# One engine for the norms', the output projections' and the second MLP matrix's adds, and two latent pairs ahead of the context

## The chip, the cores and the metric

One of the eight cores of one Trainium2 chip runs the kernel. Its engines each work through a queue of their own in order: TensorE (PE; PEld is its weight load), VectorE (DVE), ScalarE (ACT), GpSimd (POOL) and SyncE (SP), which issues the DMAs. The metric is the time of one execution on the device in microseconds; less is better. The median of three runs is given, and rows come from one profiled execution.

## What is computed

Two layers of a diffusion trunk over 1024 latent tokens and 256 context tokens, width 1024, all in float32. Layer 0 mixes by multi-head latent attention, layer 1 by gated linear attention (GLA). Cut to what matters here:

```python
for i in range(2):
    h_lat, h_ctx = modulated rms_norm of x_lat, x_ctx
    y_ctx, y_lat = mixer(h_ctx, h_lat)          # ends with "@ w_o", the output projection
    x_lat = x_lat + m_lat[:, 2] * rms_norm(y_lat, norm_g[i, 1])
    h = modulate(rms_norm(x_lat, norm_g[i, 2]), m_lat[:, 3], m_lat[:, 4])
    x_lat = x_lat + m_lat[:, 5] * rms_norm(sqrelu_mlp(h, w1[i], w2[i]), norm_g[i, 3])
    # in layer 0 the same two lines for x_ctx
def sqrelu_mlp(h, w1, w2):
    return jnp.square(jax.nn.relu(h @ w1)) @ w2   # hidden width 4096
```

## The kernel before

**Data and matmuls.** Activations lie transposed, a tile for each 128 of the 1024 channels: 128 partitions by 256 context tokens (block 0) or 512 latent tokens (blocks 1 and 2). Each float32 product is three matmuls (`mm3`, L234 to L236: high x high, high x low, low x high). Each operand is therefore split in two: ScalarE casts the high part (L204), and VectorE or GpSimd subtracts it for the low part (L201), by the engine that the call names; `alternate()` takes the two in turn. A tile's name tells its pool: `stg` and `s` come by DMA, `w` holds weight splits, `m` and `c` activations of 512 and 256 columns, `t` short-lived ones, `ps` is PSUM.

**What sets the order.** The program is written in Python for a framework that orders the instructions of each engine when it is built, by a simulated timeline, and puts in the waits. On the chip each engine keeps to that order.

**Stages.** Attention of layer 0 runs to about 700 us. The output projection (`out_proj`, `out_items`, L796 to L815; blocks 1, 0, 2) lasts to 842. For each half of the output channels it runs over eight input tiles, splits operand and weight (L804, L805) and issues the matmuls for four PSUM tiles. Then it copies each (L812), and `sumsq` (L294 to L302) squares it on ScalarE (L301) and adds it up (L302), here on GpSimd. Each block's norm, `residual_norm_steps` (L846 to L885), runs in the background behind the next block's matmuls. It calls `rstd` (L304 to L320; L309 is the matmul with ones that sums over the partitions), multiplies eight tiles by gate and rstd (L860), adds the residual (L862), stores the stream (L866, L868), squares and sums again (L301, L302), calls `rstd` once more and modulates (`modulate`, L326 to L329, or L880 with `whole`). Which engine adds at L862 is said by a table, `PLAN['radd']`, that names the tiles that go to VectorE; the others go to GpSimd.

**The first MLP matrix.** `mlp` (L891) splits the eight tiles of the latent block 1 (L898 on), waits until the context block is ready (`ready(h[0])`), and issues eight early pairs in layer 0, eleven in layer 1, by `up_early` (L975): two Strassen products of a latent pair (`top_left`), then, in layer 0, two products on the context (`up_ctx_part`). The other products follow in `up_pair`, from about 940 in layer 0.

**The second MLP matrix.** `down` (L1057 to L1149) lasts from 1215 to about 1565 in layer 0, and from 2600 to 2860 in layer 1. It is a Strassen product in five stages of sixteen steps each. A step has four `mm3`, with weights prepared two steps ahead. The weights of the stages are combinations of four blocks of the matrix, kept in one tile for each pair of rows: `s3` and `s1` in the first two stages, `w_s1` and `w_s2` in the next two, each with one add or subtract (L889) on GpSimd and a split on VectorE. `sums`, at the end of the fourth stage, has four adds for each of four output tiles, two of them on GpSimd. `ada_halves` (L268) runs between the steps. `into_ctx` (L1233) adds context products from PSUM. After `down` come `down_tail` and the norm of the block, in layer 0 from 1565 to 1680.

**GLA.** It runs from 1680 to 2250. Its output projection (`gla_wo`) and the norms of its two blocks run from about 2240, and the early pairs of layer 1 from 2318. The last norm of all lies within 2860 to 2997.

## Time and profile before

| | before |
|---|---|
| median of 3 runs | 3007.78 us (3006.51 to 3010.25) |
| profiled execution | 2998.72 us, span 2996.9 us |
| granted clock of TensorE, mean | 0.963 |
| TensorE (PE) | 2767.2 us busy, 92% |
| VectorE (DVE) | 2293.1 us, 77% |
| ScalarE (ACT) | 1599.5 us, 53% |
| GpSimd (POOL) | 1484.2 us, 50% |
| DMA | 179 GB/s mean |

The page gives busy time of each engine over the whole span. A row of the timeline has the start in us after the span's start, the time to the end of the last of its instructions, engine, line, operation, output and inputs, the shape, the count, and in brackets the idle time of the engine ahead of it and what ended that. In the tables by stage a row has the window and its length, then busy us and, in brackets, instructions of PE, PEld, DVE, ACT and POOL, then the granted clock, the DMA engines' busy share and GB/s. The two windows of the section below are the loops of the second MLP matrix in layer 0 and in layer 1. The granted clock is 1.00 for 2.4 GHz and 0.50 for 1.2 GHz.

### The profile page before, as it was taken

What the parts mean: (1) busy time and instruction counts of PE and PEld (TensorE: products, weight loads), DVE (VectorE), ACT (ScalarE), POOL (GpSimd) and SP (SyncE); (2) the same over time, 40 slices, a digit from 0 to 9 for tenths busy, and PEclk for the clock granted to TensorE, in tenths of its full rate; (3) what the DMA queues carried; (4) which work ended last, traced back from release to release, by engine and by line L of the source; (5) the groups of instructions that cost most, each with busy time, mean ns of one, the idle gap of its engine ahead of it and who ended that gap; (6) DMA issues with size and microseconds to landing.
All of it is one profiled execution on the core that took longest, in us unless ns stands there. A gap on an engine that the chain in (4) does not pass through costs nothing. (4 is left out here: it accounts for less than half of the span.)

```text
span 2996.9 us, 44715 instructions
## 1 busy us (share of the span) xinstructions
PE 2767.2 (92%) x14646; PEld 2360.5 (79%) x14646; DVE 2293.1 (77%) x3776; ACT 1599.5 (53%) x3360; POOL 1484.2 (50%) x1029
## 2 busy tenths in 40 slices
PE   6799898999889989999999999799888989999997
PEld 4678787898778778888777888688777768788877
DVE  8898999886898985576888683466898876576676
ACT  5577576665455334444435454656655644555433
POOL 5554444425634753332533252366565389664522
PEclk8999999999899999999999999899999999999999
DMA  5221334225554874487755465666576547577454
GB/s 205 69 80 58 125 109 137 90 76 175 176 172 158 262 243 144 149 286 227 237 187 173 164 204 170 213 213 226 191 261 203 197 156 238 172 270 255 146 186 144
DMA packets 319386, 535.49 MB, mean 179 GB/s; under 512 B 33073, under 2 KB 96433, under 8 KB 319153
## 3 DMA queue, kind: packets, MB, share of 16 engines
q1 hardware_dynamic: 313328, 527.39, 53.6%
q10 hardware_dynamic: 5760, 5.25, 0.5%
q8 instruction: 115, 1.88, 0.3%
q14 instruction: 119, 0.97, 0.1%
q0 software_dynamic: 64, 0.00, 0.0%
HBM read 412.18 MB, written 120.32 MB: 178 GB/s over the span
## 5 line engine op out<-in xcount | busy, mean ns | idle before, releaser
L235 PE MATMUL ps<-m,w 128*128 128x512 f32 (+1 forms) x2320 | 907.4, 392 | 25.9 <-DVE m L201 24.6
L236 PE MATMUL ps<-m,w 128*128 128x512 f32 (+1 forms) x2320 | 903.0, 392 | 29.1 <-DVE w L201 23.4
L234 PE MATMUL ps<-m,w 128*128 128x512 f32 (+1 forms) x2320 | 893.2, 394 | 28.5 <-ACT m L204 11.8
L235 PEld LDWEIGHTS ps<-m,w 128*128 128x128 f32 x2320 | 447.7, 193 | 124.7 <-DVE m L201 33.9
L236 PEld LDWEIGHTS ps<-m,w 128*128 128x128 f32 x2320 | 446.1, 193 | 124.4 <-DVE w L201 29.5
L234 PEld LDWEIGHTS ps<-m,w 128*128 128x128 f32 x2320 | 444.9, 192 | 122.9 <-ACT m L204 16.5
L204 ACT CAST w<-stg 128x512 fp32r<-128x512 f32 (+2 forms) x510 | 308.6, 613 | 273.1 <-PE ps L235 205.1
L201 POOL TENSOR_TENSOR w<-stg,w 128x512 fp32r<-128x512 f32 (+2 forms) x173 | 241.7, 1399 | 382.2 <-ACT w L204 315.6
L201 DVE TENSOR_TENSOR w<-stg,w 128x512 fp32r<-128x512 f32 x337 | 308.8, 923 | 155.9 <-ACT w L204 142.0
L204 ACT CAST m<-stg 128x512 fp32r<-128x512 f32 x296 | 177.7, 623 | 180.7 <-DMA stg<-hid 162.6
L201 DVE TENSOR_TENSOR m<-stg,m 128x512 fp32r<-128x512 f32 x220 | 199.5, 928 | 60.3 <-ACT m L204 60.0
L234 PE MATMUL ps<-m,m 128*128 128x256 f32 (+1 forms) x632 | 187.9, 317 | 28.1 <-ACT m L204 17.8
L235 PE MATMUL ps<-m,m 128*128 128x256 f32 (+1 forms) x632 | 196.1, 312 | 11.5 <-POOL m L201 7.2
L234 PE MATMUL ps<-c,w 128*128 128x256 f32 (+1 forms) x664 | 185.6, 286 | 15.6 <-ACT c L436 7.0
L236 PE MATMUL ps<-m,m 128*128 128x256 f32 (+1 forms) x632 | 192.5, 306 | 1.8 <-DVE m L427 1.8
L235 PE MATMUL ps<-c,w 128*128 128x256 f32 (+1 forms) x664 | 186.0, 284 | 6.1 <-DVE c L437 3.5
L236 PE MATMUL ps<-c,w 128*128 128x256 f32 (+1 forms) x664 | 185.7, 284 | 0.1
L965 ACT ACTIVATE t<-t 128x512 f32<-128x512 f32 x109 | 68.8, 631 | 204.8 <-DVE t L889 194.9
L889 DVE TENSOR_TENSOR t<-ps,t 128x512 f32<-128x512 f32 x164 | 111.1, 684 | 79.9 <-PE ps L236 54.6
L889 POOL TENSOR_TENSOR m<-stg,stg 128x512 f32<-128x512 f32 x64 | 95.3, 1495 | 131.2 <-DVE w L201 64.4
L234 PEld LDWEIGHTS ps<-m,m 128*128 128x128 f32 x632 | 124.2, 197 | 38.9 <-ACT m L204 19.3
L889 POOL TENSOR_TENSOR t<-t,t 128x512 f32<-128x512 f32 x82 | 123.4, 1513 | 39.8 <-issue 19.2
(312 smaller groups left out, 6490.1 us busy)
## 6 DMA issues: line engine op xcount, KB each, us to landing
stg<-in_mlp_w SPq DMA_DIRECT2D x256, 256.0 KB, 3.9
stg<-hid SPq DMA_DIRECT2D x227, 256.0 KB, 3.7
hid<-t SPq DMA_DIRECT2D x205, 256.0 KB, 3.3
stg<-in_w SPq DMA_DIRECT2D x182, 256.0 KB, 3.0
ada<-in_adaT SPq DMA_DIRECT2D x88, 512.0 KB, 3.6
stg<-in_adaT SPq DMA_DIRECT2D x112, 256.0 KB, 3.6
stg<-in_gla_wv SPq DMA_DIRECT2D x64, 256.0 KB, 3.7
stg<-in_mla_wo SPq DMA_DIRECT2D x48, 256.0 KB, 4.1
```

What stands on the lines that cost most here:

```text
L201: eng.tensor_tensor(out=out, in0=a, in1=bits(hi), op=ALU.subtract)
L204: self.nc.scalar.copy(hi, src)
L234: mm(ps, lhs[0], rhs[0], start=first, stop=False, skip_group_check=shared)
L235: mm(ps, lhs[0], rhs[1], start=False, stop=False, skip_group_check=shared)
L236: mm(ps, lhs[1], rhs[0], start=False, stop=last, skip_group_check=shared)
L889: eng.tensor_tensor(out=out, in0=a, in1=b, op=op)
L965: self.nc.scalar.activation(c, c, AF.Relu)
```

## The change

Four edits. (1) In `out_items` both splits' subtracts and the square-sums go to VectorE, in place of taking turns and of GpSimd (4 calls: 48 subtracts, 28 square-sums; `out_half_items`, the other form of gla_wo, stays). (2) All residual adds of `residual_norm_steps` are VectorE's; the table is gone (52 move). (3) In `down` the adds of `s3`, `s1`, `w_s1` and `w_s2` are VectorE's (64 in each layer), and `sums` leaves only its first add in place. The three others go into a list, and each of the following steps issues one, on VectorE (16 in both layers move engine). (4) `up_early` is cut in two. The latent part, `up_first`, is called for two pairs ahead of the wait for the context block, and their context parts, `up_first_ctx`, come after it, in the loop as before. VectorE has 3995 instructions of its program's queue after, 3724 before; GpSimd 762 and 1034.

```diff
- 'radd': [[6, 7], [6], [6, 7, 1, 2], [6, 7, 5]],
+ 'ahead': 2,
...
@@ out_items
-                    o.append(self.msplit(self.load(src[k, :, t0 - off:t0 - off + w]), w, self.alternate()))
-                ww = self.weight(self.I[wname][k * P:(k + 1) * P, half * 512:half * 512 + 512], self.alternate())
+                    o.append(self.msplit(self.load(src[k, :, t0 - off:t0 - off + w]), w, self.nc.vector))
+                ww = self.weight(self.I[wname][k * P:(k + 1) * P, half * 512:half * 512 + 512], self.nc.vector)
...
-                self.sumsq(acc, pss[n], half == 0 and n == 0, w, self.nc.gpsimd)
+                self.sumsq(acc, pss[n], half == 0 and n == 0, w)
@@ residual_norm_steps
-            (nc.vector if k in PLAN['radd'][l * 2 + (gate == 5)] else nc.gpsimd).tensor_tensor(out=ys[k], in0=ys[k], in1=xs[k], op=ALU.add)
+            nc.vector.tensor_tensor(out=ys[k], in0=ys[k], in1=xs[k], op=ALU.add)
@@ mlp
+        hc = h[0] if ctx else None
...
+        ahead = PLAN["ahead"] if ctx else 0
+        held = [self.up_first(l, p, ops) for p in range(ahead)]
         if ctx:
             self.ready(h[0])
...
         for p in range(early):
-            self.up_early(l, p, ops, hc)
+            w = held.pop(0) if held else self.up_first(l, p, ops)
+            self.up_first_ctx(l, p, w, hc)
@@ up_early, now up_first and up_first_ctx
+        return w
+
+    def up_first_ctx(self, l, p, w, hc):
         if hc:
+            V = self.nc.vector
             self.up_ctx_part(2 * p, (w["11"], w["12"]), hc)
             self.up_ctx_part(2 * p + 1, [self.weight(self.I["w1"][l, 2 * p + 1, i], V) for i in range(2)], hc)
@@ down
-            self.tt(Pl, keep[p], a11, part(p, 0, 1), ALU.subtract)
+            self.tt(V, keep[p], a11, part(p, 0, 1), ALU.subtract)
...
-            self.tt(Pl, keep[p], keep[p], part(p, 0, 0), ALU.subtract)
+            self.tt(V, keep[p], keep[p], part(p, 0, 0), ALU.subtract)
...
-            self.tt(Pl, C["u3", n], C["u3", n], u, ALU.add)
-            self.tt(Pl, u, u, C["22", n], ALU.add)
-            self.tt(V, C["22", n], C["22", n], C["u3", n], ALU.add)
+            later.extend(((C["u3", n], C["u3", n], u), (u, u, C["22", n]), (C["22", n], C["22", n], C["u3", n])))
...
             if p % 3 == 0:
                 self.ada_halves(1)
+            if later:
+                self.tt(V, *later.pop(0), ALU.add)
```

Three places in the order of the instructions; a name is a pool's letter with two running numbers.

TensorE at the end of the output projection of layer 0, before (ps2355 is its last tile, m2384 the sum of squares of the context block, m2410 and m2411 the first latent operand of the MLP):

```order
L234 MATMUL ps2355_9632<-m2339_9586,w2398_9833 128x512
L235 MATMUL ps2355_9632<-m2340_9587,w2398_9833 128x512
L236 MATMUL ps2355_9632<-m2339_9586,w2399_9834 128x512
L309 MATMUL ps2426_9914<-m2384_9770,ones_70 128x256
L234 MATMUL ps2460_9985<-m2410_9882,w2453_9973 128x512
L235 MATMUL ps2460_9985<-m2411_9883,w2453_9973 128x512
L236 MATMUL ps2460_9985<-m2410_9882,w2454_9974 128x512
```

and after, from the same tile on:

```order
L234 MATMUL ps2355_9632<-m2339_9586,w2398_9833 128x512
L235 MATMUL ps2355_9632<-m2340_9587,w2398_9833 128x512
L236 MATMUL ps2355_9632<-m2339_9586,w2399_9834 128x512
L234 MATMUL ps2434_9928<-m2410_9882,w2427_9916 128x512
L234 MATMUL ps2435_9942<-m2418_9898,w2430_9922 128x512
L234 MATMUL ps2444_9974<-m2410_9882,w2437_9962 128x512
L234 MATMUL ps2445_9988<-m2418_9898,w2440_9968 128x512
L235 MATMUL ps2434_9928<-m2411_9883,w2427_9916 128x512
```

and 44 rows later:

```order
L234 MATMUL ps2445_9988<-m2424_9910,w2440_9968 128x512
L235 MATMUL ps2445_9988<-m2425_9911,w2440_9968 128x512
L236 MATMUL ps2445_9988<-m2424_9910,w2441_9969 128x512
L309 MATMUL ps2446_10006<-m2384_9770,ones_70 128x256
L234 MATMUL ps2472_10063<-c2449_10017,w2427_9916 128x256
L234 MATMUL ps2480_10104<-c2449_10017,w2475_10094 128x256
```

48 matmuls of the two latent pairs stand between the projection and L309 now, and the first matmul on a context operand (c2449) comes right behind L309.

VectorE at the norm of latent block 2 behind the second MLP of layer 0, before, from the seventh of the eight L860 on (m3325 is a context product that `into_ctx` adds to, w4163 a weight split of `down_tail`):

```order
L860 SCALAR_TENSOR_TENSOR m3881_16384<-m3881_16384,m005_80,m4133_17357 128x512
L860 SCALAR_TENSOR_TENSOR m3882_16389<-m3882_16389,m005_80,m4133_17357 128x512
L889 TENSOR_TENSOR m3325_14241<-m3325_14241,ps4151_17461 128x256
L201 TENSOR_TENSOR w4163_17496<-stg4155_17481,w4162_17495 128x512
L201 TENSOR_TENSOR w4209_17712<-stg4203_17701,w4208_17711 128x512
```

and after:

```order
L860 SCALAR_TENSOR_TENSOR m3881_16384<-m3881_16384,m005_80,m4133_17357 128x512
L860 SCALAR_TENSOR_TENSOR m3882_16389<-m3882_16389,m005_80,m4133_17357 128x512
L889 TENSOR_TENSOR m3325_14241<-m3325_14241,ps4151_17461 128x256
L201 TENSOR_TENSOR w4163_17496<-stg4155_17481,w4162_17495 128x512
L862 TENSOR_TENSOR m3999_16834<-m3999_16834,s4128_17335 128x512
L862 TENSOR_TENSOR m4000_16839<-m4000_16839,s4129_17337 128x512
L201 TENSOR_TENSOR w4209_17712<-stg4203_17701,w4208_17711 128x512
L862 TENSOR_TENSOR m4001_16844<-m4001_16844,s4130_17339 128x512
L862 TENSOR_TENSOR m4002_16849<-m4002_16849,s4131_17341 128x512
```

The eight L860 keep their place, and four residual adds (L862) now come in VectorE's queue, behind the context's L889 and the split w4163.

VectorE at the norm behind gla_wo, before, from the seventh of its eight L860 on (w6143 is a weight split of gla_wo):

```order
L860 SCALAR_TENSOR_TENSOR m5973_24727<-m5973_24727,m102_88,m6078_25170 128x512
L860 SCALAR_TENSOR_TENSOR m5975_24732<-m5975_24732,m102_88,m6078_25170 128x512
L862 TENSOR_TENSOR m5888_24375<-m5888_24375,s6068_25138 128x512
L862 TENSOR_TENSOR m5890_24380<-m5890_24380,s6069_25140 128x512
L201 TENSOR_TENSOR w6143_25419<-stg6141_25416,w6142_25418 128x512
L302 TENSOR_TENSOR m6091_25225<-m6091_25225,t6094_25237 128x512
L302 TENSOR_TENSOR m6091_25225<-m6091_25225,t6102_25269 128x512
```

and after:

```order
L860 SCALAR_TENSOR_TENSOR m5973_24727<-m5973_24727,m102_88,m6078_25170 128x512
L860 SCALAR_TENSOR_TENSOR m5975_24732<-m5975_24732,m102_88,m6078_25170 128x512
L862 TENSOR_TENSOR m5887_24372<-m5887_24372,s6067_25136 128x512
L862 TENSOR_TENSOR m5888_24375<-m5888_24375,s6068_25138 128x512
L201 TENSOR_TENSOR w6143_25419<-stg6141_25416,w6142_25418 128x512
L862 TENSOR_TENSOR m5890_24380<-m5890_24380,s6069_25140 128x512
L862 TENSOR_TENSOR m5892_24385<-m5892_24385,s6070_25142 128x512
L201 TENSOR_TENSOR w6148_25446<-stg6146_25443,w6147_25445 128x512
```

Two residual adds stand ahead of w6143 both times: before those of the second and third tile (m5888, m5890), now those of the first and second. The next two stand behind it now; the one of the fourth tile (m5892) was GpSimd's.

## Rows read from the trace of the kernel before

**Rows 1.** The page: busy us of an engine, share of the span, instructions.

```profile
PE 2767.2 (92%) x14646; PEld 2360.5 (79%) x14646; DVE 2293.1 (77%) x3776; ACT 1599.5 (53%) x3360; POOL 1484.2 (50%) x1029
```

**Rows 2.** Table by stage: window, busy us of PE, PEld, DVE, ACT, POOL, clock, DMA.

```profile
1215.00:1565.00 350.00, 338.32 (x1712) 287.54 (x1711) 257.82 (x444) 151.98 (x289) 137.79 (x92) 0.98 0.69 225
...
2600.00:2860.00 260.00, 260.00 (x1149) 215.29 (x1148) 177.19 (x205) 127.01 (x220) 140.96 (x95) 1.00 0.65 218
```

**Rows 3.** Timelines of DVE and POOL where the other is idle: start, us, instruction.

```profile
794.63 1.07 DVE L812 COPY m<-ps 128x256 f32<-128x256 f32 x3
795.63 0.68 DVE L862 TENSOR_TENSOR m<-m,s 128x512 f32<-128x512 f32 x1
796.23 0.68 DVE L201 TENSOR_TENSOR w<-stg,w 128x512 fp32r<-128x512 f32 x1
...
2337.61 5.38 DVE L860 SCALAR_TENSOR_TENSOR m<-m,m,m 128x512 f32<-128x512 f32 x8
...
2343.07 1.29 POOL L862 TENSOR_TENSOR m<-m,s 128x512 f32<-128x512 f32 x1 [16.68 <-DVE m L860]
```

**Rows 4.** Timelines of DVE and POOL at the norms and the sums, where both work.

```profile
774.93 11.52 DVE L860 SCALAR_TENSOR_TENSOR m<-m,m,m 128x512 f32<-128x512 f32 x8
...
1531.56 6.81 DVE L201 TENSOR_TENSOR m<-stg,m 128x512 fp32r<-128x512 f32 x4
...
1590.04 12.53 DVE L860 SCALAR_TENSOR_TENSOR m<-m,m,m 128x512 f32<-128x512 f32 x8
1595.29 8.41 POOL L862 TENSOR_TENSOR m<-m,s 128x512 f32<-128x512 f32 x5
...
2274.46 10.59 DVE L860 SCALAR_TENSOR_TENSOR m<-m,m,m 128x512 f32<-128x512 f32 x8
2288.33 1.75 DVE L201 TENSOR_TENSOR w<-stg,w 128x512 fp32r<-128x512 f32 x1
...
2358.06 1.30 DVE L862 TENSOR_TENSOR m<-m,s 128x512 f32<-128x512 f32 x1 [1.82 <-DMA s<-x_scr]
...
2898.02 12.64 DVE L860 SCALAR_TENSOR_TENSOR m<-m,m,m 128x512 f32<-128x512 f32 x8
```

**Rows 5.** Timeline of PE: its idle time ahead of the row in brackets.

```profile
804.82 2.04 PE L309 MATMUL ps<-m,ones 128*128 128x512 f32 x2 [4.37 <-DVE m L302]
...
854.72 1.22 PE L309 MATMUL ps<-m,ones 128*128 128x256 f32 x2 [13.14 <-DVE m L302]
...
1602.95 0.58 PE L234 MATMUL ps<-c,w 128*128 128x256 f32 x1 [6.90 <-DVE m L889]
...
2290.14 1.22 PE L236 MATMUL ps<-m,w 128*128 128x512 f32 x2 [4.29 <-DVE w L201]
...
2323.63 0.80 PE L235 MATMUL ps<-m,w 128*128 128x512 f32 x1 [3.62 <-DVE m L201]
...
2364.57 2.08 PE L309 MATMUL ps<-m,ones 128*128 128x512 f32 x2 [4.41 <-DVE m L302]
...
2912.38 0.58 PE L235 MATMUL ps<-m,w 128*128 128x512 f32 x1 [2.88 <-DVE m L201]
```

**Rows 6.** Table by stretch, four intervals at half clock, columns as in rows 2.

```profile
803.20:810.00 6.80, 5.18 (x10) 3.48 (x11) 3.78 (x4) 2.87 (x5) 3.76 (x3) 0.50 0.72 239
...
1598.50:1608.80 10.30, 5.85 (x21) 5.35 (x22) 10.30 (x14) 3.61 (x7) 6.05 (x5) 0.50 0.66 198
2288.00:2294.80 6.80, 4.66 (x11) 3.69 (x12) 6.59 (x5) 3.39 (x6) 6.59 (x4) 0.50 0.89 286
...
2912.70:2916.10 3.40, 3.40 (x9) 2.65 (x8) 3.40 (x7) 0.92 (x2) 0.00 (x0) 0.50 0.70 202
```

**Rows 7.** Timeline of PE: first matmul on context operands of the first MLP.

```profile
862.20 0.40 PE L234 MATMUL ps<-c,w 128*128 128x256 f32 x2
```

**Rows 8.** Waits of PE from 1420 to 1620: us in total, times, longest us.

```profile
PE ps L235 <- DVE m L201: 10.5, 4, 5.3
```

**Rows 9.** Waits of POOL from 1200 to 1600, columns as in rows 8.

```profile
POOL m L889 <- DMA stg<-in_mlp_w: 50.5, 14, 13.1
```

More of the change, by code (lines that the diff above doesn't have):

```diff
@@ L897, in mlp @@
             ops["11" if k < 4 else "21"].append(self.msplit(h[1][k], 512, self.nc.vector))
+        hc = h[0] if ctx else None
+        second = self.strassen_y(ops, h[1], h[2])
+        ahead = PLAN["ahead"] if ctx else 0
+        held = [self.up_first(l, p, ops) for p in range(ahead)]
         if ctx:
             self.ready(h[0])
-        hc = h[0] if ctx else None
-        second = self.strassen_y(ops, h[1], h[2])
         for p in range(early):
-            self.up_early(l, p, ops, hc)
+            w = held.pop(0) if held else self.up_first(l, p, ops)
+            self.up_first_ctx(l, p, w, hc)
             self.tick(PLAN["etick"][l])
@@ L973, in top_left, with up_first @@
         return a, c
-    def up_early(self, l, p, B, hc):
+    def up_first(self, l, p, B):
         V = self.nc.vector
@@ L1064, in down @@
         nc = self.nc
-        Pl, V = nc.gpsimd, nc.vector
-        keep = {}
+        V = nc.vector
+        keep, later = {}, []
         def part(p, r, i):
@@ L1072, in s3 @@
             keep[p] = self.m()
-            self.tt(Pl, keep[p], a11, part(p, 0, 1), ALU.subtract)
+            self.tt(V, keep[p], a11, part(p, 0, 1), ALU.subtract)
         def s1(p, a21):
-            self.tt(Pl, keep[p], a21, part(p, 1, 1), ALU.add)
+            self.tt(V, keep[p], a21, part(p, 1, 1), ALU.add)
         def w_first(p):
@@ L1096, in w_s2 @@
             w = self.wsplit(keep[p], V)
-            self.tt(Pl, keep[p], part(p, 1, 0), keep[p], ALU.subtract)
+            self.tt(V, keep[p], part(p, 1, 0), keep[p], ALU.subtract)
             return w, None
```

## The prediction

> **What bounds the kernel now.** I read the page first. TensorE is busy 92% of the span [rows 1], so what can be won without removing matmuls is its idle time, some 230 us, and the stretches after an idle time in which its clock is at half. VectorE is busy 77%. The table by stage comes next. In the second MLP product of layer 1 TensorE is busy for all 260 us while VectorE has 177 us of work, and in that of layer 0 it is 338 of 350 with VectorE at 258 [rows 2]. So there is room on VectorE in those stages, and in layer 1 nothing can be won.
>
> Then the timelines of VectorE and GpSimd, side by side. A run of eight L860 takes 5.38 us where GpSimd is idle, 0.67 apart, and instructions with two operands of 512 columns start 0.60 apart (795.63, 796.23), copies of 256 columns 0.33 apart (three in 1.07) [rows 3]. The same eight L860 take 10.6 to 12.6 us where GpSimd adds the residuals beside them, and five such GpSimd adds take 8.41, so 1.68 each, against 1.29 for one alone [rows 4]. So the two engines hold each other up: while both work on SBUF operands, VectorE does in 1.5 us what it does in 0.6 to 0.7 alone. An add moved from GpSimd to VectorE then costs VectorE 0.60, and saves the 0.9 that its neighbours lost to it.
>
> Last the idle times of TensorE, row by row, with what ended them [rows 5]. Seven are 2.9 to 13.1 us long, all seven were ended by VectorE, and all lie in or right behind an output projection or a residual norm. Behind them the granted clock is 0.50, the lower of its two levels (1.2 GHz of 2.4): in the four intervals shown for 3.4 to 10.3 us. What that costs is half of TensorE's busy time in it: 2.6, 2.9, 2.3 and 1.7 us [rows 6].
>
> **The change part by part.** It moves 272 instructions from GpSimd to VectorE: 48 subtracts and 28 square-sums of the output projections, 52 residual adds, 144 adds of the second MLP product. It removes none, and TensorE and ScalarE keep theirs (one instruction more in TensorE's queue, at nothing).
>
> *Output projections, layer 0.* The idle time of 4.37 us at 804.82 ends with the second norm's sum [rows 5]. Its last square-sum is on VectorE behind 11.5 us of L860. In the new order 42 instructions stand from the first L860 to that sum, eight at 0.67, 26 at 0.60, eight of 256 columns at 0.33: (5.4 + 15.6 + 2.6) = 23.6 us from 774.9, so 798.5, ahead of 804.82 − 4.37 = 800.45, where TensorE ran out. Idle time and half clock go: 4.4 + 2.6 = 7.0 saved. The shorter wait at the start of that block stays, since the queue before the operand gained as many instructions as each got shorter.
>
> *Two latent pairs ahead.* The idle time of 13.14 at 854.72 is TensorE waiting with L309 for the sum over the context block, with the first MLP's matmuls queued behind [rows 5]. In the new order 48 matmuls of the two pairs stand ahead of it (48 x 0.226 = 10.9 us, by 1149 matmuls in 260 us [rows 2]). But they wait for the operand splits of the latent block, and these stand in VectorE's queue behind six instructions of 512 columns and five of 256, (6 x 0.60 + 5 x 0.33) = 5.3 us. And then the context's chain, from L309 at 854.72 to the first matmul on context operands at 862.20, 7.5 us [rows 5, 7], lies open: today 24 latent matmuls run inside it, and these have been used up. Less the first sum itself and what the chain loses to splits that stand between its steps today, 5.5 to 6.5 us of it are idle. So 5.3 ahead and some 6 behind take the place of 13.14: −2. With the wait in two pieces there may be a second half-clock stretch, so I take no clock gain here. If the operands come sooner than I count, the bound is the whole 13.1 plus 1.5 of clock.
>
> *Second MLP, layer 0.* 72 adds move to VectorE: 258 + 72 x 0.60 = 301 us of 350, before what the missing contention gives back, so it doesn't become the bound by load. Four waits for VectorE's operand splits, 10.5 us in all, the longest 5.3 [rows 8]. The 5.3 is that of the sums at the end of the product: now four L889, then splits at 1.7 each (three in 5.11) beside GpSimd's adds [rows 4]; then four plus three L889 and two splits, 9 x 0.60 = 5.4. Nothing won there. The other three, 5.2 in all, sit behind contended splits; I take 3 of it and 1.5 of clock (below the smallest interval of rows 6, as two of the three are short): −4.5.
>
> *Residual norm of the layer-0 MLP.* The largest: 6.90 idle at 1602.95, ended by L889 (into_ctx) that stands behind the eight L860 of 12.53 us [rows 4, 5]. In the new order the eight L860 stand alone, 8 x 0.67 = 5.4, to which two GpSimd splits of the tail's weights may still add 0.9 each. L889 then ends at 1590.04 + 5.4 + 1.8 + 0.4 = 1597.6, TensorE ran out at 1596.05. So 5.3 to 6.9 of idle time and the clock's 2.9 go: −8.5.
>
> *Layer 1: gla_wo and norms.* w6143, the weight split for which TensorE waits 4.29 us, runs at 2288.33, behind eight L860 of 10.59 and two adds [rows 4, 5]. After: one more split, eight at 0.67, two at 0.60 and its own 0.68 from 2274.46, so 2282.3, before TensorE runs out at 2290.14 − 4.29 = 2285.85: 4.3 + 2.3 of clock = −6.6. The wait of 3.62 at 2323.63 is for operand splits beside GpSimd square-sums, which move: −1. The one of 4.41 at 2364.57 looks alike, but the add at 2358.06 was itself waiting for the load of the residual (1.82, DMA) [rows 4], and that load comes when an earlier add frees its buffer. Earlier adds bring it forward by 2 us, not more: −2. At the last norm eight L860 take 12.64 and the operand split behind them is 2.88 late [rows 4, 5]: −2.9 − 1.7 = −4.6. The second MLP of layer 1 is full on TensorE, with 177 + 43 of 260 on VectorE afterwards [rows 2]: nothing.
>
> *What may come in its place.* An add on GpSimd that waits (for a residual or a weight by DMA) held up only GpSimd's queue. On VectorE it holds up the operand splits behind it, and TensorE after them. GpSimd's adds of the second MLP in layer 0 waited 50.5 us for weights by DMA, in 14 waits [rows 9]. The bounds are 0 (VectorE gets to them later than GpSimd did, the data is there) and 50.5. VectorE is at 301 of 350 and TensorE's work is prepared two steps ahead, so I am near the lower end: +6.
>
> Sum: −7.0 − 2 − 4.5 − 8.5 − 6.6 − 1 − 2 − 4.6 = −36.2, and +6: **−30 us**. The profiled execution took 2998.7 in its own time, and the median of three is 9 us above it; the difference is put on the median: 3007.8 − 30 = **2978**.
>
> **A rule that speaks against it.** The rows have VectorE's instructions of 0.68 us start 0.60 apart, one behind the other [rows 3]. The Trainium skill (VectorE: DVE Perf Modes, "The DRAIN you can't avoid") says that each VectorE instruction is followed by a drain of about its duration less 266 ns before the next starts, but also that one which isn't held starts earlier. By the first half an instruction would take 0.68 + 0.41 = 1.09, the 144 adds of the second MLP 157 us in place of 86, and the sum would be about −30 + 71 = +41. The trace doesn't agree with that pace, so the sum stays as it is.
>
> **The rivals.** (1) *Half of it comes.* The waits lie in VectorE's one queue, and an earlier L860 only exposes the next wait: a residual's load (as at 2358.06), a ScalarE cast, a square. For it: the wait at 2364.57 is of that kind already. Against: for the largest terms the queue is counted through, and the loads are not late there. Then −15, 2993. (2) *VectorE inherits GpSimd's waits* in the layer-0 second MLP: the adds stand in its queue ahead of the splits, and wait for weights. If most of the 50.5 us reaches TensorE, the time is 3007.8 − 30 + 50.5 = 3028; it decides once more than 36 of the 50.5 come through, from there on the kernel is slower by over 6. Against it: TensorE has two prepared steps, 5.4 us, ahead, and the 14 waits are 3.6 us on average. (3) *Nothing that can be measured*: the half above, and a few waits of rival 2 (12 us) beside it, 3005. (4) *VectorE doesn't run the moved adds at 0.60.* Other GpSimd work moves up beside them, and each holds VectorE for some 1.1 us, between the 0.60 of rows 3 and the 1.5 of rows 4: the 144 adds of the second MLP cost 72 us more, layer 1's stage included (177 + 79 of 260), and the time is 3049. The drain of the Trainium skill would give the same; the pace in rows 3 is against it.
>
> **How the numbers follow.** About 0.2% (6 us) is what a measurement of this kernel can tell from no change. Forecast, 2978: 0.60, its own range 2955 to 2989. Half, 2993: 0.22. No difference, 3005: 0.08. Slower by GpSimd's inherited waits, 3028: 0.09; by adds at 1.1 us, 0.01. The lower bound is the sum without the +6 and with the whole of the 13.1 and its clock: −36.2 − 12.6 = −49, and 5 for splits that run free in stretches I didn't count: 2953. The upper end takes in the half gain with some loss, up to 3002; what lies above is 0.15, below 0.05. Faster 0.82, same 0.08, slower 0.10.
>
> **What would show it.** Runs of eight L860 of 5.4 to 7 us at all four norms; TensorE's idle times at 804, 1596, 2286 and 2910 gone and the granted clock at 1.0 there; at 842 two waits of about 5 us, one on the operand splits and one on context operands, in place of 13; the second MLP of layer 1 unchanged at TensorE's pace. I am wrong if VectorE's L889 adds show waits for weight DMAs with TensorE idle behind them, or if VectorE's share in the layer-0 second MLP nears 95%, or if the L860 stay at 1.5 us each because other GpSimd work has moved up into their place.

## The result and the profile after

The changed kernel takes 2971.6 us (median of 4 runs, 2968.3 to 2973.7); the kernel before took 3007.2 beside it (4 runs, 3001.0 to 3010.3). The ratio is 0.9887, 95% interval 0.9869 to 0.9905: 36 us less, forecast 30. The profiled execution of after took 2972.39 (span 2970.6), near its median, while that of before was 8 us below its own (and 2 below the lowest of the four). The two traces therefore differ by 26 us and not by 36; of what follows, the shares are of the 26.

The page of after, first line of its part 1 (as rows 1):

```profile
PE 2761.4 (93%) x14646; PEld 2358.3 (79%) x14646; DVE 2265.1 (76%) x4048; ACT 1603.6 (54%) x3360; POOL 1092.3 (37%) x757
```

GpSimd goes from 50% to 37% of the span. VectorE has 272 instructions more and is busy 28 us less: 2265 in place of 2293. The table by stage has the same for the second MLP (as rows 2; each window runs between the same two matmuls of TensorE as there, which come earlier now):

```profile
1208.61:1550.73 342.12, 336.20 (x1712) 286.57 (x1712) 250.28 (x516) 153.44 (x289) 29.10 (x20) 0.99 0.70 230
...
2576.89:2836.89 260.00, 260.00 (x1149) 215.29 (x1148) 184.26 (x277) 127.92 (x220) 33.38 (x23) 1.00 0.65 220
```

In both layers VectorE has the 72 moved instructions more than in rows 2; in layer 0 it has 7.5 us less work for that, in layer 1 7 us more. At 0.60 us each (rows 3) the 72 are 43 us, so they gave back some 51 and 36 us by the way: 0.7 and 0.5 us for each moved add, an estimate, where the prediction had 0.9. The groups by line and form show where it comes from. First before, then after (mean ns of one behind the busy time):

```profile
L860 DVE SCALAR_TENSOR_TENSOR m<-m,m,m 128x512 f32<-128x512 f32 x56 | 69.7, 1313 | 0.1
L201 DVE TENSOR_TENSOR m<-stg,m 128x512 fp32r<-128x512 f32 x220 | 199.5, 928 | 60.3 <-ACT m L204 60.0
L889 DVE TENSOR_TENSOR t<-ps,t 128x512 f32<-128x512 f32 x164 | 111.1, 684 | 79.9 <-PE ps L236 54.6 <-DMA hid<-t 8.7 <-POOL t L889 7.5
```

```profile
L860 DVE SCALAR_TENSOR_TENSOR m<-m,m,m 128x512 f32<-128x512 f32 x56 | 43.0, 836 | 0.0
L201 DVE TENSOR_TENSOR m<-stg,m 128x512 fp32r<-128x512 f32 x244 | 173.7, 724 | 55.1 <-ACT m L204 53.9 <-DMA stg<-in_mlp_w 0.6
L889 DVE TENSOR_TENSOR t<-ps,t 128x512 f32<-128x512 f32 x164 | 111.2, 684 | 86.2 <-PE ps L236 51.4 <-DMA hid<-t 16.5 <-POOL t L889 8.2
```

Instructions with two SBUF operands get shorter, L860 from 1313 to 836 ns and the operand subtract from 928 to 724. One that reads PSUM and SBUF takes 684 both times. As the GpSimd work beside that group was not moved, the trace of before has to show it by itself: 54 of the 164 run beside GpSimd instructions for over 95% of their time and take 683 ns on average, 76 run with GpSimd idle and take 684. Of the 56 L860, 29 beside GpSimd for as much of theirs take 1770, 19 with GpSimd idle 747. The Trainium skill (SBUF — State Buffer, "Who interferes with whom") says that a VectorE instruction contends with GpSimd's reads when both its inputs are in SBUF, and, outside its two-port modes, not with at most one; these numbers agree on both halves.

Five runs of L860 at the norms of layer 0 and of layer 1, timelines of VectorE (as rows 4):

```profile
775.36 5.38 DVE L860 SCALAR_TENSOR_TENSOR m<-m,m,m 128x512 f32<-128x512 f32 x8
...
1575.76 7.46 DVE L860 SCALAR_TENSOR_TENSOR m<-m,m,m 128x512 f32<-128x512 f32 x8
...
2261.56 5.38 DVE L860 SCALAR_TENSOR_TENSOR m<-m,m,m 128x512 f32<-128x512 f32 x8
...
2319.39 5.38 DVE L860 SCALAR_TENSOR_TENSOR m<-m,m,m 128x512 f32<-128x512 f32 x8
...
2874.92 7.46 DVE L860 SCALAR_TENSOR_TENSOR m<-m,m,m 128x512 f32<-128x512 f32 x8
```

5.38 where GpSimd is idle, 7.46 where it still splits two weights of a tail. And TensorE's idle times around the places of rows 5, with two that are new (1400.32 and 2905.91):

```profile
783.16 1.94 PE L234 MATMUL ps<-m,w 128*128 128x512 f32 x4 [2.58 <-ACT m L204]
788.14 0.80 PE L235 MATMUL ps<-m,w 128*128 128x512 f32 x1 [3.03 <-DVE m L201]
...
838.68 1.65 PE L234 MATMUL ps<-m,w 128*128 128x512 f32 x3 [2.19 <-ACT m L204]
...
857.57 0.79 PE L234 MATMUL ps<-c,w 128*128 128x256 f32 x2 [4.65 <-ACT c L328]
...
1400.32 0.50 PE L236 MATMUL ps<-m,w 128*128 128x512 f32 x1 [3.10 <-DVE w L201]
...
1583.61 0.38 PE L234 MATMUL ps<-c,w 128*128 128x256 f32 x1 [3.16 <-DVE m L889]
...
2304.80 0.80 PE L235 MATMUL ps<-m,w 128*128 128x512 f32 x1 [5.22 <-DVE m L201]
...
2342.34 1.23 PE L309 MATMUL ps<-m,ones 128*128 128x512 f32 x2 [1.92 <-DVE m L302]
...
2905.91 0.38 PE L234 MATMUL ps<-c,m 128*128 128x256 f32 x1 [3.42 <-ACT m L204]
```

The idle time of 4.37 at 804 is gone, and so are the 4.29 at 2290 and the 2.88 at 2912. 13.14 has become 2.19 and 4.65, 6.90 has become 3.16, 4.41 has become 1.92. The 5.22 at 2304 is larger than the 3.62 it answers to. The two at 783 and 788 were there before as well (4.09 and 1.28).

The start of the same matmul in both traces, place by place, gives the ledger of the 26 us. The last column is the same for a second copy of the changed program ("The sums in place" below), and shows how far two executions of one order of instructions differ:

| stage | forecast | trace of after | second copy |
|---|---|---|---|
| output projection, to its last matmul | −7.0 | −7.0 | −6.7 |
| pairs ahead, to 940 | −2 | −1.4 | −2.0 |
| rest of the first MLP | 0 | +1.6 | +2.8 |
| second MLP, layer 0, up to the sums | −4.5 | −0.6 | −4.8 |
| the sums | 0 | −7.3 | −7.3 |
| norm and tail, layer 0 | −8.5 | −2.4 | −3.1 |
| GLA | 0 | −0.1 | −4.6 |
| gla_wo, to the early pairs | −7.6 | −2.9 | −1.2 |
| second norm there | −2 | −3.4 | −3.2 |
| second MLP, layer 1 | 0 | 0.0 | +0.4 |
| last norm | −4.6 | −3.2 | −2.9 |
| new waits (not placed) | +6 | in the rows above | in the rows above |
| up to the output projection (unchanged code) | 0 | +0.4 | +4.6 |
| sum | −30 | −26.3 | −28.1 |

The norms, the output projections and the sums repeat within 2 us. Three of the stretches between them don't: up to the output projection, in the second MLP ahead of the sums and in GLA one program differs by more than 4 us from itself, so nothing smaller can be read there from one trace.

### The profile page after: what moved, and what is told of

Read it like the earlier page. It is cut to its first block, busy times and chain, and to the rows that moved or that the text cites. A ratio compares the mean times of both kernels' runs of the same rounds, so it can differ in the third digit from the quotient of the medians.

```text
span 2970.6 us, 44564 instructions
## 1 busy us (share of the span) xinstructions
PE 2761.4 (93%) x14646; PEld 2358.3 (79%) x14646; DVE 2265.1 (76%) x4048; ACT 1603.6 (54%) x3360; POOL 1092.3 (37%) x757
## 5 line engine op out<-in xcount | busy, mean ns | idle before, releaser
L235 PE MATMUL ps<-m,w 128*128 128x512 f32 (+1 forms) x2320 | 906.7, 392 | 20.7 <-DVE m L201 20.2
L236 PE MATMUL ps<-m,w 128*128 128x512 f32 (+1 forms) x2320 | 899.2, 391 | 28.3 <-DVE w L201 22.5
L234 PE MATMUL ps<-m,w 128*128 128x512 f32 (+1 forms) x2320 | 891.4, 394 | 30.1 <-ACT m L204 13.2
L236 PEld LDWEIGHTS ps<-m,w 128*128 128x128 f32 x2320 | 445.5, 193 | 123.6 <-DVE w L201 28.3
L235 PEld LDWEIGHTS ps<-m,w 128*128 128x128 f32 x2320 | 447.1, 193 | 115.9 <-DVE m L201 28.1
L201 POOL TENSOR_TENSOR w<-stg,w 128x512 fp32r<-128x512 f32 (+2 forms) x157 | 220.4, 1406 | 818.5 <-ACT w L204 747.2
L201 DVE TENSOR_TENSOR w<-stg,w 128x512 fp32r<-128x512 f32 x353 | 280.5, 798 | 154.0 <-ACT w L204 136.5
L201 DVE TENSOR_TENSOR m<-stg,m 128x512 fp32r<-128x512 f32 x244 | 173.7, 724 | 55.1 <-ACT m L204 53.9
L234 PE MATMUL ps<-m,m 128*128 128x256 f32 (+1 forms) x632 | 187.3, 316 | 29.5 <-ACT m L204 18.6
L235 PE MATMUL ps<-m,m 128*128 128x256 f32 (+1 forms) x632 | 195.6, 311 | 10.4 <-POOL m L201 5.9
L234 PE MATMUL ps<-c,w 128*128 128x256 f32 (+1 forms) x664 | 186.4, 288 | 16.6 <-ACT c L436 7.1
L236 PE MATMUL ps<-m,m 128*128 128x256 f32 (+1 forms) x632 | 192.0, 305 | 1.8 <-DVE m L427 1.8
L235 PE MATMUL ps<-c,w 128*128 128x256 f32 (+1 forms) x664 | 185.4, 283 | 5.9 <-DVE c L437 3.5
L236 PE MATMUL ps<-c,w 128*128 128x256 f32 (+1 forms) x664 | 184.7, 283 | 0.0
L889 DVE TENSOR_TENSOR t<-ps,t 128x512 f32<-128x512 f32 x164 | 111.2, 684 | 86.2 <-PE ps L236 51.4
L889 POOL TENSOR_TENSOR t<-t,t 128x512 f32<-128x512 f32 x82 | 124.3, 1525 | 73.0 <-DVE t L889 29.3
L234 PEld LDWEIGHTS ps<-c,w 128*128 128x128 f32 x664 | 125.4, 192 | 22.0 <-ACT c L436 7.5
```

The costliest lines, as they stand in the source:

```text
L201: eng.tensor_tensor(out=out, in0=a, in1=bits(hi), op=ALU.subtract)
L234: mm(ps, lhs[0], rhs[0], start=first, stop=False, skip_group_check=shared)
L235: mm(ps, lhs[0], rhs[1], start=False, stop=False, skip_group_check=shared)
L236: mm(ps, lhs[1], rhs[0], start=False, stop=last, skip_group_check=shared)
L889: eng.tensor_tensor(out=out, in0=a, in1=b, op=op)
```

## The experiments

The theory: VectorE and GpSimd hold each other up on SBUF operands, VectorE's queue runs late for that, and TensorE waits for operands in it. The rivals: the gain comes from the order of the queues (GpSimd's adds were in the chain), from the two pairs ahead, or from the late sums. Each run was timed beside the kernel before; the ratio is to that.

| kernel | median us | runs | ratio, 95% interval |
|---|---|---|---|
| residual adds alone | 2994.2 | 6 | 0.9959 (0.9944 to 0.9975) |
| output projections alone | 3005.3 | 11 | 1.0003 (0.9993 to 1.0013) |
| second MLP's adds and late sums alone | 2996.8 | 6 | 0.9966 (0.9950 to 0.9982) |
| two pairs ahead alone | 3016.4 | 6 | 1.0034 (1.0023 to 1.0046) |
| residual adds and output projections | 2987.0 | 5 | 0.9938 (0.9926 to 0.9951) |
| change without the pairs ahead | 2972.5 | 4 | 0.9897 (0.9881 to 0.9913) |
| the change | 2971.6 | 4 | 0.9887 (0.9869 to 0.9905) |
| change with GpSimd adds beside L860 | 3009.3 | 11 | 1.0015 (1.0006 to 1.0025) |
| change with the sums in place | 2968.7 | 4 | 0.9875 (0.9860 to 0.9890) |
| change, tails on VectorE | 2967.2 | 4 | 0.9867 (0.9851 to 0.9884) |
| change, gla_wo halves on VectorE | 2968.9 | 4 | 0.9877 (0.9856 to 0.9898) |
| change, adaT a step ahead | 2971.7 | 4 | 0.9884 (0.9867 to 0.9900) |
| change, tails and gla_wo halves, sums in place | 2961.4 | 5 | 0.9852 (0.9830 to 0.9873) |

**GpSimd put back, with no one waiting for it.** The change with a useless GpSimd add beside each L860.

```diff
+                self.dump = self.pool.tile([P, 448], F32, name="dump")
...
         for k in range(KT):
+            nc.gpsimd.tensor_tensor(out=self.dump[:, :min(w, 448)], in0=r[:, :min(w, 448)], in1=r[:, :min(w, 448)], op=ALU.add)
             nc.vector.scalar_tensor_tensor(out=ys[k], in0=ys[k], scalar=self.co(l, s, gate, k), in1=r,
```

> The changed kernel with one GpSimd add beside each L860 of every norm (448 or 256 columns, both inputs the norm's rstd tile, the result never read); the order on the four other engines is the same. Nobody waits for these adds but later GpSimd work. Theory (the engines slow each other on SBUF operands): the eight L860 take 10 us or more again, and 10 to 19 us of the gain go, 2982 to 2991. Rival (the gain comes from the order of the queues, GpSimd's adds being out of the chain): within 3 us of the changed kernel.

Measured: 3009.3, ratio 1.0015 in place of 0.9887, so 38 us more than the change; all of its gain is gone, at least twice what was expected. VectorE, TensorE, ScalarE and SyncE have the change's queues, instruction for instruction. Timelines of VectorE and GpSimd at the first latent norm, and the group of L860 in this kernel:

```profile
779.58 10.80 DVE L860 SCALAR_TENSOR_TENSOR m<-m,m,m 128x512 f32<-128x512 f32 x8
...
778.86 10.96 POOL L860 TENSOR_TENSOR dump<-m 128x448 f32<-128x448 f32 x8 [69.80 <-DVE m L320]
```

```profile
L860 DVE SCALAR_TENSOR_TENSOR m<-m,m,m 128x512 f32<-128x512 f32 x56 | 75.1, 1407 | 0.0
```

```profile
L860 POOL TENSOR_TENSOR dump<-m 128x448 f32<-128x448 f32 x56 | 70.2, 1253 | 189.9 <-DVE m L320 186.6
```

Eight L860 are back at 10.80, and their mean is 1407 ns in place of 836. That adds 32 us of VectorE time over the 56 of 512 columns, which lies at the places where TensorE waits for what stands behind it. TensorE's waits from 775 to 875, this kernel first and the change below it (us in total, times, longest):

```profile
PE ps L234 <- ACT m L204: 13.6, 3, 8.0
```

```profile
PE ps L234 <- ACT m L204: 5.8, 3, 2.6
```

The longest, 8.0, ends with a ScalarE cast. That stands in ScalarE's queue behind a square (L298) that waits for a residual add, which stands behind the slow L860 on VectorE (0.8 in the change):

```profile
ACT m L298 <- DVE m L862: 6.3, 1, 6.3
```

The queue rival falls: its order is that of the change and its time that of before. Another one would be that the useless adds hold up GpSimd's own later work. The waits speak against it: those of TensorE that GpSimd ends are 16.6 us in all in this kernel and 18.6 in the change, those of VectorE 54.7 and 53.8.

The ledger, this trace against that of the change, places the loss: 4.8 us at the output projection of layer 0, 9.3 from there to 940, 4.3 at the norm behind the MLP, 4.5 at gla_wo, 5.4 at the second norm there and 5.0 at the last norm, together 33 of the 33.5 by which the traces differ. (Of the rest, 5.0 up to the output projection and −4.8 in the second MLP cancel.) I had priced the return by the ledger of the change, and at most of these places more comes back than the change had won there. That it is more because in this kernel VectorE has slow L860 and its own residual adds, where in the kernel before GpSimd did the adds that slowed them, is only argued.

**The parts alone.** Residual adds:

```diff
-            (nc.vector if k in PLAN['radd'][l * 2 + (gate == 5)] else nc.gpsimd).tensor_tensor(out=ys[k], in0=ys[k], in1=xs[k], op=ALU.add)
+            nc.vector.tensor_tensor(out=ys[k], in0=ys[k], in1=xs[k], op=ALU.add)
```

> The kernel before with the residual adds of the norms on VectorE and nothing else. Theory (VectorE and GpSimd slow each other on SBUF operands): eight L860 take 5.4 to 7.5 us in place of 10.6 to 12.6 at the norms behind both MLPs and gla_wo; TensorE's idle times of 6.90 (L889, layer-0 tail), 4.29 (w split at gla_wo) and 2.88 (last norm) shrink to 3.2, 0.4 and 0, as in the changed kernel. That kernel's trace gives 2.5 + 3.4 + 3.3 + 3.2 us for the four places, so 12 us less than before, up to 16 with a part of the output projection's 6.6. Rival (moved adds wait in VectorE's queue for the residual's load and push the splits behind them): within 4 us of before or slower, with VectorE's L862 waiting for DMA.

Measured 12 us less, as expected.

Output projections:

```diff
-                    o.append(self.msplit(self.load(src[k, :, t0 - off:t0 - off + w]), w, self.alternate()))
+                    o.append(self.msplit(self.load(src[k, :, t0 - off:t0 - off + w]), w, self.nc.vector))
...
-                self.sumsq(acc, pss[n], half == 0 and n == 0, w, self.nc.gpsimd)
+                self.sumsq(acc, pss[n], half == 0 and n == 0, w)
```

> The kernel before with the splits and square-sums of the output projections on VectorE and nothing else; GpSimd still adds the residuals. Theory: the eight L860 at 775 still run beside six GpSimd adds, so they still take 10 us or more, and VectorE now has 24 more instructions there: TensorE's idle time of 4.37 us at L309 stays or grows, and the time is within 4 us of before. Rival (it is the splits and sums on GpSimd that make TensorE wait there): the 6.6 us of the stage are won by this part alone.

Measured: no change. Both parts:

```diff
-            (nc.vector if k in PLAN['radd'][l * 2 + (gate == 5)] else nc.gpsimd).tensor_tensor(out=ys[k], in0=ys[k], in1=xs[k], op=ALU.add)
+            nc.vector.tensor_tensor(out=ys[k], in0=ys[k], in1=xs[k], op=ALU.add)
...
-                self.sumsq(acc, pss[n], half == 0 and n == 0, w, self.nc.gpsimd)
+                self.sumsq(acc, pss[n], half == 0 and n == 0, w)
```

> The kernel before with the residual adds and the output projections on VectorE, the first MLP and the second as before. Theory (the wait of 4.37 at 804 goes only when both kinds of GpSimd work have left the eight L860): the 12 us of the adds alone and 5 to 7 at the output projection, 2986 to 2990, so more than the two parts on their own (12 and 1). Rival (the two parts just add): 2993 or above.

Measured 18 us less, so 5 more than 12 and 1. The timelines of TensorE show what each part leaves at the first norm. With the residual adds alone, then with the projections alone:

```profile
785.16 1.22 PE L234 MATMUL ps<-m,w 128*128 128x512 f32 x4 [2.55 <-ACT m L204]
789.32 0.79 PE L235 MATMUL ps<-m,w 128*128 128x512 f32 x1 [2.95 <-POOL m L201]
...
805.05 1.19 PE L309 MATMUL ps<-m,ones 128*128 128x512 f32 x1 [3.73 <-DVE m L302]
```

```profile
776.20 11.53 DVE L860 SCALAR_TENSOR_TENSOR m<-m,m,m 128x512 f32<-128x512 f32 x8
...
793.32 0.79 PE L235 MATMUL ps<-m,w 128*128 128x512 f32 x1 [9.58 <-DVE m L201]
```

With the adds moved L860 runs free, but the sum is still partly on GpSimd, and TensorE waits 3.73 for it at 805. With the projections moved the wait for the sum is gone, but L860 still takes 11.53, and weight splits and copies stand behind it, so that TensorE waits 9.58 for an operand. My expectation had the wait at 804 stay; with the projections alone it moved. TensorE's waits at this norm come to 9.7 us before, 9.2 and 10.7 with one part, 6.2 with both.

By the starts of its matmuls this stage still wins 2.3 and 2.6 us with one part and 6.7 with both, so only a part of the surplus arises here. More of it lies at gla_wo and the norm behind it (2240 to 2375 of before), which the expectation didn't name: +0.9 and +3.9 us with one part, −8.5 with both. The wait for the second norm's sum there, with the residual adds alone, the projections alone, and both:

```profile
2364.41 2.08 PE L309 MATMUL ps<-m,ones 128*128 128x512 f32 x2 [3.58 <-DVE m L302]
```

```profile
2372.12 1.22 PE L309 MATMUL ps<-m,ones 128*128 128x512 f32 x1 [6.64 <-DVE m L302]
```

```profile
2351.24 1.13 PE L309 MATMUL ps<-m,ones 128*128 128x512 f32 x2 [1.50 <-DVE m L302]
```

Second MLP:

```diff
-            self.tt(Pl, keep[p], a11, part(p, 0, 1), ALU.subtract)
+            self.tt(V, keep[p], a11, part(p, 0, 1), ALU.subtract)
...
-            self.tt(Pl, C["u3", n], C["u3", n], u, ALU.add)
-            self.tt(Pl, u, u, C["22", n], ALU.add)
-            self.tt(V, C["22", n], C["22", n], C["u3", n], ALU.add)
+            later.extend(((C["u3", n], C["u3", n], u), (u, u, C["22", n]), (C["22", n], C["22", n], C["u3", n])))
```

> The kernel before with the adds of the second MLP product on VectorE and the late sums, nothing else. Theory: the wait of 5.3 us at the sums in layer 0 goes with its half-clock stretch, 7.3 us as in the changed kernel; the rest of the stage stays within 1 us, since a wait of about 3 us behind an adaT load stands against what the other splits gain: 6 to 9 us less than before. Rival (VectorE inherits GpSimd's 50.5 us of waits for weights): slower by up to 30 us.

Measured 10 us less, 7.3 of it in the trace at the sums. The inherited waits don't come: nothing is slower.

The sums in place, from the change:

```diff
-            later.extend(((C["u3", n], C["u3", n], u), (u, u, C["22", n]), (C["22", n], C["22", n], C["u3", n])))
+            self.tt(V, C["u3", n], C["u3", n], u, ALU.add)
+            self.tt(V, u, u, C["22", n], ALU.add)
+            self.tt(V, C["22", n], C["22", n], C["u3", n], ALU.add)
```

> The changed kernel with all four adds of each sum in place, on VectorE, none late. Theory (the wait at the sums goes because the later adds no longer stand ahead of the next operand splits): 16 adds of 0.60 stand in a row, 9.6 us, TensorE has two prepared steps of 2.7, and a wait of 3 to 5 us with a half-clock stretch returns in layer 0, in layer 1 too: 4 to 12 us slower than the changed kernel. Rival (it went because GpSimd no longer runs beside the splits there): within 2 us of the changed kernel.

Measured 2968.7, 3 us below the change. The order of all five engines is that of the change, instruction for instruction: the framework spreads these adds by itself, and the list changes nothing. So this run is a second copy of the changed program, and 3 us is what two copies differ by here. So the wait at the sums goes with the move to VectorE in this stage and not with the list; which of the stage's adds it takes, and whether by the missing contention or by the new order of VectorE's queue, was not tried. In the queue of VectorE in the change, the sums and the first splits behind them:

```profile
1513.97 1.28 DVE L889 TENSOR_TENSOR m<-ps,m 128x512 f32<-128x512 f32 x2
...
1517.57 0.68 DVE L889 TENSOR_TENSOR m<-m,m 128x512 f32<-128x512 f32 x1
1518.17 0.68 DVE L201 TENSOR_TENSOR w<-m,w 128x512 fp32r<-128x512 f32 x1
1518.77 0.68 DVE L201 TENSOR_TENSOR m<-stg,m 128x512 fp32r<-128x512 f32 x1
```

The first sum starts 13.9 us ahead of before's (1527.84 there); the stage stands 7.0 earlier in this trace, so VectorE comes to the sums 6.9 us earlier relative to TensorE.

Two pairs ahead:

```diff
+        held = [self.up_first(l, p, ops) for p in range(ahead)]
         if ctx:
             self.ready(h[0])
```

> The kernel before with two latent pairs ahead of the context block and nothing else. Theory: the idle time of 13.14 us at 842 splits into one on the latent operands and one of about 5 us on the context's operands, and since the norms' adds still run beside each other the first is longer than the 3.2 us of the changed kernel: 0 to 4 us less than before. Rival (the two pairs fill the wait): 10 to 13 us less.

> The changed kernel without the two pairs ahead (table entry 0), so the three engine moves together. Theory by the changed kernel's ledger (the pairs won 1.4 us there): 0 to 4 us slower than the changed kernel, 2972 to 2976, with one idle time of 8 to 11 us at L309 in place of two of 3.2 and 4.7. Rival (the pairs cost what they cost alone, 10 us): about 2962.

Measured: with the pairs alone 10 us slower than before; without them 1 us slower than the change, inside the spread. TensorE's waits from 840 to 945 with the pairs alone, and from 830 to 945 with the three engine moves and no pairs:

```profile
PE ps L236 <- DVE m L202: 6.3, 2, 4.8
PE ps L235 <- ACT m L205: 3.2, 1, 3.2
PE ps L310 <- DVE m L303: 2.6, 1, 2.6
```

```profile
PE ps L309 <- DVE m L302: 13.2, 1, 13.2
```

(In the first kernel the lines stand one further down, L236 for L235.) Alone, the pairs' matmuls wait for the latent splits, which run contended (the longest 4.8). Trace against trace, 5.4 us come from 841 to 940 of before, 8 more up to 1560 and nothing after. Of those 8, 3.5 come from 940 to 1215; the kernel with the second MLP's adds alone, whose code up to there is that of before, loses as much there, so the trace of before is a quick one in that stretch. The other 4.5 are not explained. Without the pairs the one wait of 13.2 is there in full. From 830 on that kernel loses 1.7 us to the change by 870 and 3.2 by 1215, and wins 9 behind that, in stages whose code is the same. (In the second copy GLA alone wins 4.5, see the ledger.) So the pairs' 1.4 to 1.7 us are seen at their place and not in the medians, and the 10 us that they cost alone don't come in the change.

**What is left on GpSimd.** Three more kernels move or shift something in the change. The weight splits of the second MLP's tails and the last norm's adds, on VectorE:

```diff
-        return [self.wsplit(x, self.alternate()) for x in xs]
+        return [self.wsplit(x, self.nc.vector) for x in xs]
...
-                    W[p] = self.msplit(self.w2(l, 2 * p + 1, 1), 512, self.alternate())
+                    W[p] = self.msplit(self.w2(l, 2 * p + 1, 1), 512, self.nc.vector)
...
-                (nc.vector if k in PLAN["ladd"] else nc.gpsimd).tensor_tensor(out=x, in0=ys[k], in1=x, op=ALU.add)
+                nc.vector.tensor_tensor(out=x, in0=ys[k], in1=x, op=ALU.add)
```

> The changed kernel with the weight splits of the second MLP's tails and the last norm's adds on VectorE too (table ladd and both alternations there). Theory: the eight L860 behind both second MLPs take 5.4 us in place of 7.46, the idle time of 3.16 at L889 in layer 0 shrinks to about 1, and no GpSimd split takes 3 us in the last tail: 2 to 6 us less than the changed kernel, so 2966 to 2970. Rival (VectorE is the longer queue there and gets more to do): no change or up to 5 us slower.

Measured 2967.2. The two halves of the L860 in layer 0 take 2.73 each with a split between them, and the L889 is waited for 1.7 us in place of 3.2. The time is 4 us lower, but two copies differ by 3. The trace is clearer at one place: the wait of 3.42 at 2905.91, which is 3.7 to 5.9 in four more kernels that have the change (without the pairs, sums in place, gla_wo halves, adaT), is gone, and the last norm takes 5.7 us less than in the change.

The splits and square-sums of gla_wo's halves, on VectorE:

```diff
-                ww = self.weight(self.I["gla_wo"][k * P:(k + 1) * P, half * 512:half * 512 + 512], self.alternate())
+                ww = self.weight(self.I["gla_wo"][k * P:(k + 1) * P, half * 512:half * 512 + 512], self.nc.vector)
...
-                self.sumsq(acc[:, c], pss[n], half == 0 and n == 0, 256, self.nc.gpsimd)
+                self.sumsq(acc[:, c], pss[n], half == 0 and n == 0, 256)
```

> The changed kernel with the splits and square-sums of gla_wo's half blocks on VectorE too. Theory: the sum's wait for GpSimd (1.35 at 2252) goes and what runs beside the halves gets free: 1 to 4 us less than the changed kernel. Rival (the stage waits for ScalarE's casts and loads): within 1 us.

Measured 2968.9: not told from the spread.

The adaT halves loaded one step ahead of the reduction that reads them:

```diff
+            if pend:
+                self.ada_reduce(*pend)
+                pend = None
             if p % 3 == 0:
-                self.ada_halves(1)
+                pend = self.ada_load()
```

> The changed kernel with the second MLP's adaT halves loaded one step ahead of the VectorE reduction that reads them. Theory (the new idle time of 3.10 at 1397 is a weight split queued behind a reduction that waits 2.3 us for its adaT load): that idle time and its half clock go, 3 to 5 us in layer 0: 2967 to 2969, and VectorE's waits for adaT there fall from 24 us to under 10. Rival (the split is late by the hidden tile's load and cast): no change, another instruction shows the wait.

Measured 2971.7, no change. The idle time at 1397 stays at 2.95, and VectorE still waits 22 us in 16 waits for the adaT halves. From the issue of such a load to its reduction there are 4.8 us in this stage, 5.0 in the change (medians of 56). So the step written into the program didn't put distance between load and reduction on the chip, and the theory of that stall isn't tried by it.

The last kernel has the edits of the tails, gla_wo's halves and the sums together.

```diff
-        return [self.wsplit(x, self.alternate()) for x in xs]
+        return [self.wsplit(x, self.nc.vector) for x in xs]
...
-                self.sumsq(acc[:, c], pss[n], half == 0 and n == 0, 256, self.nc.gpsimd)
+                self.sumsq(acc[:, c], pss[n], half == 0 and n == 0, 256)
```

> The changed kernel with the tails' and gla_wo's splits and square-sums on VectorE too and with the sums' adds in place. Theory: the parts' 4, 3 and 3 us add up, being in different stages: 2960 to 2965, 7 to 11 us less than the changed kernel. Rival (each of the three was within its spread): 2967 to 2972.

Measured 2961.4: 10 us below the change, and each of its five runs (2958.2 to 2966.6) below the change's lowest, though not below the lowest of its second copy (2962.9). In its trace the two largest steps against the change at these places are 5.5 us at the last norm, where the wait of 3.42 is gone as with the tails alone, and 2.8 at gla_wo (the 5.22 of 2304 is 2.85 there). It is faster than both kernels.

## Why the prediction was right, and where not

**The mechanism** was right: the useless adds show it apart from any order. The size was near, 30 against 36, but by terms that missed in both directions; that they cancel is luck.

**Output projection** (−7.0): as counted. L860 takes 5.38, and the sum is there before TensorE needs it.

**Two pairs** (−2): the split of the wait came as described, 3.2 ahead (1.00 and 2.19) and 4.65 behind in place of 5.3 and some 6, with half-clock stretches behind each. −1.4 and −2.0 in the ledger, nothing in the medians.

**Second MLP, layer 0**: here a step failed, at the sums. "Nothing won there" at the sums was a count of the queue from where VectorE began them, 9 x 0.60 = 5.4. But the wait was not the length of that queue. VectorE itself came to it 6.9 us late, and that lateness went. In the trace of before seven of its instructions between 1499 and 1520 take 1.1 us longer than others of their kind (the L268 at 1508.60 takes 1.77, that at 1510.91 0.68), which would make it up; no run shows it apart from the order. (The pace given there, "three in 5.11", stands in rows 4 as four in 6.81.) The −4.5 for the three other waits can't be decided from one trace. In that of after it is −0.6, since the new idle time of 3.10 at 1400 takes 4.9 us with its clock. It is that of a weight split queued behind a reduction that waits for its adaT load:

```profile
1398.96 0.69 DVE L268 CUSTOM_DVE_ANT_0 stg<-stg,cl 128x512 f32<-128x512 f32 x1 [2.33 <-DMA stg<-in_adaT]
1399.58 0.69 DVE L201 TENSOR_TENSOR w<-m,w 128x512 fp32r<-128x512 f32 x1
```

That the split stands behind it is read from the queue. But the second copy, with the same order, has no idle time at this place and −4.8 in the ledger, and the kernel with the useless adds none either, and −5.4; in the other kernels with these adds on VectorE it is 1.2 to 3.1 us long. So this idle time comes and goes between executions, and −4.5 lies within what they show.

**Norm of layer 0** (−8.5, traces −2.4 and −3.1): the step that failed is where TensorE runs out. VectorE's part came as counted: the eight L860 take 7.46, and the L889 ends 7.9 us behind their start, 12.9 before. But TensorE ran out 4.7 us behind that start and not 6.0, so the idle time went from 6.90 to 3.16 only. Then a wait of 1.96 for operand splits followed at 1589, with a half-clock stretch.

**gla_wo** (−7.6, traces −2.9 and −1.2): the 4.29 went. But by the place of 2284 in the trace of before, just ahead of it, 3.6 us had been lost, by a new wait of 1.35 at 2252 for the sum, which GpSimd still does, and by a longer stretch at half clock behind it: 6.8 us from 2254.5, against 3.4 from 2270.95 before. (A wait of 1.95 for a cast between the two is in both traces.) And the 3.62 became 5.22: VectorE now runs eight L880 (5.39 from 2295.15) where TensorE needs the operand splits. GpSimd is idle there, so this is the order, not contention.

**Last norm** (−4.6, −3.2) and **second norm** (−2, −3.4): right within 2 us. At the last norm the 2.88 went as counted, and the 3.42 at 2905.91 came, where before has 2.11 at 2938.83.

**New waits** (+6): they came, at gla_wo, at 1589, at the last norm and, in this trace, at 1400, and not from GpSimd's waits for weights. So the size was near and the reason given for it was not what happened. Of the 50.5 us VectorE inherits 2.6, in four waits of L889 for `in_mlp_w` from 1200 to 1600:

```profile
DVE m L889 <- DMA stg<-in_mlp_w: 2.6, 4, 1.2
```

**The rivals.** "VectorE inherits GpSimd's waits" fell by that row. "Half of it comes" was right of single terms, not of the sum. The pace of 1.1 us fell: the moved instructions start 0.60 apart (1517.57, 1518.17, 1518.77 in the sums above). The drain that the Trainium skill tells of (VectorE: DVE Perf Modes, "The DRAIN you can't avoid") doesn't show between these instructions; the page says itself that one which isn't held starts earlier.

**Parts and whole.** Adds alone −12, projections alone −1, second MLP alone −10 make −23; together they give −33 (3005.1 to 2972.5), which is just outside what the intervals of the four ratios allow. A part that leaves GpSimd's other work beside VectorE leaves a part of the wait, here or at the next norm.

## What to carry to other kernels

Where two engines slow each other on SBUF operands, the price of an instruction is what it takes plus what it takes from its neighbour. Compare the same instruction's mean with the other engine idle and busy before giving work to an idle engine, and test it with useless work on that engine that nobody waits for. Moving one part of such work out of a stretch can give little while the other part stays. Before a new idle time of a few us gets a cause, see whether a second execution of the same program has it too. And where an engine is late, ask how late it comes to its queue before counting the queue.

## What the runs showed of the hardware that was not expected

Two engines are not slowed to the sum of their times. Beside GpSimd's adds of 448 columns, eight L860 take 10.80 us and the eight adds 10.96; both kinds start 1.34 apart, an L860 is 1.42 long and an add 1.26. Alone, L860 start 0.67 apart, and such an add takes 0.93, as the first one at gla_wo's norm in the same kernel, where VectorE is idle:

```profile
2276.59 0.93 POOL L860 TENSOR_TENSOR dump<-m 128x448 f32<-128x448 f32 x1 [6.42 <-DVE m L320]
```

One behind the other a pair would take 1.60, and it takes 1.34. In the kernel before, beside residual adds of 512 columns (1.29 alone, rows 3), it would be 1.96, and a pair takes 1.68 (rows 4). So VectorE's time doubles or more, and GpSimd's adds get a third longer (0.93 to 1.26, 1.29 to 1.72): a pair takes what GpSimd needs alone and 0.4 us. The Trainium skill (SBUF — State Buffer, "Who interferes with whom") calls the ports that the two engines share an exclusive lock. In these pairs it isn't held for the whole of an instruction, or they would take the sum.
